# A two-layer diffusion backbone on one core: a gated tile's low part cut and moved, half of the last head's transposed blocks in other buffers, a gate tile loaded later

## The chip, the cores and the metric

The kernel runs on one core of one Trainium2 chip. The metric is the device time of one execution in microseconds (us). TensorE (PE in the profile) multiplies matrices, VectorE (DVE), ScalarE (ACT) and GpSimd (POOL) work element by element, SyncE (SP) issues the transfers between the chip's main memory and the on-chip memory (SBUF). Matmul results stand in PSUM, which is cut into banks of 512 fp32 columns on 128 partitions. Each engine runs its own instructions in their order, and semaphores order the engines among each other.

## The reference

Each of two layers modulates and normalizes the input, projects it once to all queries, keys, values and gates, runs two attentions side by side, and merges them:

```python
def _merge(a_att, b_att, a_z, b_z, g_a, g_b, w_o_a, w_o_b, w_out):
    o_a = (a_att * jax.nn.silu(a_z)) @ w_o_a
    o_b = (b_att * jax.nn.silu(b_z)) @ w_o_b
    merged = jax.nn.sigmoid(g_a) * o_a + jax.nn.sigmoid(g_b) * o_b
    return merged @ w_out
...
    a_att = _na_latent(qa, ka, va, cka, cva, rpb, rows)
...
    b_att = _gqa_latent(qb, k_all, v_all)
    out_x = _merge(a_att, b_att, a_z, b_z, g_a, g_b, w_o_a, w_o_b, w_out)
    x_new = x + gate_x * out_x
```

`_na_latent` is a neighbourhood attention with 8 heads, `_gqa_latent` a full attention with 8 query heads on 2 key/value heads. There are 512 latent tokens and 256 context tokens of width 1024, heads of 64. Layer 0 also updates the context (768 tokens in all); layer 1 does not, and gives the 512 latent tokens out. All is fp32.

## The kernel before

**Numbers in two parts.** Every fp32 operand of a large product is split into a high part (cast to a TensorE format, on ACT) and a low part (the difference, on DVE or POOL). One product is three matmuls: high by high (L352), high by low and low by high (L353, L354 in either role). `mm3` issues them. A slab of weights is loaded into a staging buffer `raw` (three of them), cast into `whi` on ACT and subtracted into `wlo` on DVE or POOL in turn; `load_w2` (L327 to L341) does that for 256 columns, two rows of 128 at once. `whi` and `wlo` are rings of eight buffers each, handed out in program order and shared by all weights.

**The second attention.** `pipeline` runs eight heads. For head h it makes the scores (L719, L720, banks `pss`: a ring of two of 1024 columns), the softmax (exponent L958 on ACT, the division L657 on DVE or L659 and L660 on POOL), and then the values of head h-1 (`gq_values`). The values of a head need the softmax result transposed: in six blocks of 128 keys, `transpose_split` sets four transposes (L670) into one bank of a ring of two (`pst`, kind "t"), casts the block's high part into `pth` on ACT (L673) and subtracts its low part into `ptl` on DVE (L674); two buffers of each. Two matmuls per block (L973, L974) add up in the one bank `psv`. `head_out` then copies half of it to a single buffer `ho` on ACT (L682), adds the other half on DVE (L683), and multiplies the result into the gate tile `zb` on POOL (L684), which makes it the second gated tile. In layer 0 the 256 context queries go through the same path (L747, L748).

**What fills the gaps.** Between heads the pipeline issues pieces of other work from a list: gate projections and the first branch's output projection with `w_o_a` (psf matmuls with `gah` and `gal`, evacuated at L593).

**The end of a layer's attention.** When the eight heads' scores are issued, `early()` (L985) loads two gate tiles, `tg[1]` and `tg[3]`, takes two large buffers for the second gated tile's parts (`gbh`, `gbl`; from `big`, a ring of nine buffers of 128x3072), and splits three quarters of it by `hilo` (L555: cast L558 on ACT, subtraction L559 on POOL). Then come the last head's values. Then the merge takes the PSUM banks anew (five of a kind "x" beside "f"), loads the output gate, splits the last quarter, and runs over four chunks of `w_o_b`: `chunks[i][0]()` loads two slabs of weights, `chunks[i][1]` holds the matmuls (psf and psx with `gbh`, `gbl`) and `evac_b` (L1006), which joins both branches in the gate tiles and splits the result into `mh` and `ml`. After it, `w_out` multiplies that (loaded by `load_w`, L317 to L326).

**What sets the order.** The program gives the instructions in the order above; a scheduler then sets each engine's order by its own planned times, and buffers of a ring are handed out in program order, each when the reader of what stood in it before is done. So the changed kernel's order on each engine isn't read from the code, but from the built program.

Of the kernel before, what the change touches and what calls it, by code (L numbers as in the profile page):

```python
# [9 lines left out]
F32R = mybir.dt.float32r  # L10
BF16 = mybir.dt.bfloat16
AF = mybir.ActivationFunctionType
ALU = mybir.AluOpType
# [46 lines left out]
def R(ap):  # L60
    return ap.bitcast(F32R)
# [7 lines left out]
def hybrid_kernel(es: ExitStack, tc, x, ctx, cvec, w_ada, w_ada0, small, gvec, w_in, w_o_a, w_o_b, w_out,  # L69
                  bias_int, bias_edge, rope, ident_d, out):  # L70
    nc = tc.nc
    V, S, G, T = nc.vector, nc.scalar, nc.gpsimd, nc.tensor
# [3 lines left out]
    wp = es.enter_context(tc.tile_pool(name="wp", bufs=8))  # L76
# [6 lines left out]
    def nm(s):  # L83
        uid[0] += 1
        return f"{s}_{uid[0]}"

    def big(name):
        return bigp.tile([128, 3072], F32, tag="big", name=nm(name))
# [23 lines left out]
    def psw(n=512, kind="w"):  # L112
        if kind == "w":
            kind = "f" if pm["i"] % pm["n"] == 0 else "x"
            pm["i"] += 1
        pool, cols = pm[kind]
        return pool.tile([128, cols], F32, tag=kind, name=nm("ps" + kind))[:, :n]
# [290 lines left out]
    def run(fill, n):  # L408
        for _ in range(min(n, len(fill))):
            fill.pop(0)()  # L410
# [80 lines left out]
    def layer(l, hx, nxt, mid):  # L491
# [60 lines left out]
        def hilo_tiles(name):  # L552
            return [big(name + part).rearrange("p (f n) -> p f n", f=4) for part in "hl"]

        def hilo(src, dst, fs):  # L555
            sv = src.rearrange("p (f n) -> p f n", f=4)
            for f in fs:
                S.copy(R(dst[0][:, f, :ntok]), sv[:, f, :ntok])  # L558
                G.tensor_tensor(R(dst[1][:, f, :ntok]), sv[:, f, :ntok], dst[0][:, f, :ntok], ALU.subtract)  # L559

        def load_tg(c):
            nc.sync.dma_start(tg[c].rearrange("p (f n) -> p f n", f=4)[:, :, :ntok], gs[c][:, :, :ntok])
# [88 lines left out]
        if True:  # L651
# [10 lines left out]

            def transpose_split(blocks, n0=0, n1=512):

                pt = psw(512, "t")
                for src, c0 in blocks:
                    if c0 is None:
                        T.transpose(pt.rearrange("p (s n) -> p s n", n=64)[:, 0:8:7, :], src, ident)
                    else:
                        T.transpose(pt[:, c0:c0 + 128], src, ident)  # L670
                hi = att["p"].tile([128, 512], F32R, tag="pth", name=nm("pth"), bufs=att["nt"])
                lo = att["p"].tile([128, 512], F32R, tag="ptl", name=nm("ptl"), bufs=att["nt"])
                S.copy(hi[:, n0:n1], pt[:, n0:n1])  # L673
                V.tensor_tensor(lo[:, n0:n1], pt[:, n0:n1], F(hi[:, n0:n1]), ALU.subtract)  # L674
                return hi, lo

            def head_out(po, e, dst):

                n = dst.shape[-1]
                m, o = 64 * e, 64 * (1 - e)  # L680
                t1 = att["p"].tile([128, 512], F32, tag="ho", name=nm("ho"), bufs=1)
                S.copy(t1[m:m + 64, :n], po[o:o + 64, :n])  # L682
                V.tensor_tensor(t1[m:m + 64, :n], po[m:m + 64, :n], t1[m:m + 64, :n], ALU.add)  # L683
                G.tensor_tensor(dst, dst, t1[m:m + 64, :n], ALU.mult)  # L684

            def rows(a, half):
                return a[64 * half:64 * half + 64]
# [150 lines left out]
            def pipeline(fill, spread, scores_of, values_of, last=None, bg=[]):  # L838

                n = len(fill)  # L840
                prev = None
                for h in range(8):
                    att["bg"] = bg if h > 3 or pm["n"] == 1 else []
                    st = scores_of(h)
                    if prev is not None:
                        values_of(h - 1, prev)
                    run(fill, len(fill) - (n - n * min(h + 1, spread) // spread))
                    prev = st
                if last is not None:
                    run(fill, len(fill))  # L850
                    last()
                run(bg, len(bg))
                values_of(7, prev)
                run(fill, len(fill))

            akt = [k_tile(e, True) for e in range(2)]

            def na_first(h):
                j, e = h // 2, h % 2
# [6 lines left out]
            def values_of(dst, f):  # L866
                def g(h, st):
                    vsl = f(h, st[0])
                    if first:
                        e = h % 2  # L870
                        zv = dst.rearrange("p (f n) -> p f n", f=4)
                        ctx_values(st[1], vsl, zv[64 * e:64 * e + 64, h // 2, 512:768], e)
                return g
# [110 lines left out]

            def early():  # L985

                for c in (1, 3):
                    tg[c] = big("tg")
                    load_tg(c)
                gated["b"] = hilo_tiles("gb")  # L990
                hilo(zb, gated["b"], range(3))
            bg = gate_steps((1,), att["p"]) if first else []
# [3 lines left out]
        with tc.tile_pool(name=f"mrg{l}", bufs=1, reuse_waits="tile") as mp:  # L996
# [3 lines left out]
            for v in range(nv):  # L1000
                src = gd[l][8 * v:8 * v + 8].rearrange("k p -> (k p)").unsqueeze(0)
                nc.sync.dma_start(gv[:, v, :], src.to_broadcast([128, DM]))
            hilo(zb, gated["b"], [3])
            mg = []

            def evac_b(f, n0, n1, ps):  # L1006
# [8 lines left out]
            for i in range(4):  # L1015
                if i < 3:
                    chunks[i + 1][0]()
                if i % 2 == 0:
                    mg.append(hilo_tiles("m"))
                for piece in chunks[i][1]:  # L1020
                    piece()
# [225 lines left out]
```

## Time and profile before

| | us |
|---|---|
| three runs of before | 1146.18, 1144.71, 1144.48 (median 1144.71) |
| the profiled execution | 1144.91 |
| its span in the profile | 1143.1 |
| idle time of DVE before `ptl` L674, all 176 of the kernel | 43.4 |
| idle time of ACT before `pth` L673, all 176 | 93.2 |

The span is what the profile records from the first instruction to the last; 1.8 us of the profiled execution lie around it. A row of the timeline has the start, the duration, the engine, the line, the operation, what is written and from what, the shape and the count, and in brackets the idle time ahead of it with the engine and the tile that ended it. A matmul's recorded duration overlaps the next one's, so two starts tell more than a duration. The kernel has 6128 matmuls and transposes, and the context part of layer 1 is left out by the reference itself.

### The profile page before, as it was taken

How to read it: one execution, taken by the hardware profiler on the slowest of the kernel's cores; microseconds unless marked ns; L12 is line 12 of the kernel's file. 1: busy time of each engine (PE TensorE's matmuls, PEld its weight loads, DVE VectorE, ACT ScalarE, POOL GpSimd, SP SyncE). 2: the span in 40 equal slices, each digit the busy share in tenths (PEclk: the TensorE clock that was granted, in tenths of full speed). 3: DMA queues.
4: the chain of work that ended last, by engine and by line, in shares of the span. 5: the costliest groups of instructions: out<-in, count | busy, mean ns of one | idle time of the engine just before them, and what ended most of it. 6: DMA issues, size and time to landing. Idle time of an engine off the chain costs nothing.

```text
span 1143.1 us, 17425 instructions
## 1 busy us (share of the span) xinstructions
PE 1120.7 (98%) x6128; PEld 947.6 (83%) x6128; DVE 816.3 (71%) x1535; ACT 581.4 (51%) x1185; POOL 480.6 (42%) x449
## 2 busy tenths in 40 slices
PE   7999999999999999999999999999999999999998
PEld 5788888888988888888788787888887888887787
DVE  6777688887554786697588655469777665898573
ACT  6553366665443565666330355337666355766521
POOL 1073354553364333453511226345453664465311
PEclk9999999999999999999999999999999999999999
DMA  9645212333323232451434424633332333152133
GB/s 368 241 123 157 85 56 70 99 116 97 118 94 97 96 101 86 98 217 38 152 124 134 148 69 122 186 103 116 99 114 65 111 103 102 65 175 92 64 126 97
DMA packets 91886, 135.08 MB, mean 118 GB/s; under 512 B 10804, under 2 KB 55064, under 8 KB 91160
## 3 DMA queue, kind: packets, MB, share of 16 engines
q1 hardware_dynamic: 91520, 133.87, 36.9%
q8 instruction: 48, 0.79, 0.3%
q14 instruction: 38, 0.31, 0.1%
q10 hardware_dynamic: 280, 0.12, 0.0%
HBM read 116.63 MB, written 17.32 MB: 117 GB/s over the span
## 4 chain that ended last, share of the span: by engine, by line
PE 87%; DVE 5%; DMA 2%; ACT 2%; issue 2%; POOL 1%; SPq 0%; ACTq 0%; POOLq 0%; DVEq 0%
PE psx L352 12%; PE psx L354 12%; PE psx L353 12%; PE psf L352 10%; PE psf L353 10%; PE psf L354 10%; PE pst L670 5%; PE pss L792 3%; PE pss L719 2%; PE pss L720 2%; PE psv L974 2%; PE psv L973 1%; PE pst L432 1%; DVE ptl L674 1%; DMA rawb<-in_w_ada_dram 1%
## 5 line engine op out<-in xcount | busy, mean ns | idle before, releaser
L674 DVE TENSOR_TENSOR ptl<-pst,pth 128x512 fp32r<-128x512 f32 (+1 forms) x176 | 115.9, 671 | 43.4 <-ACT pth L673 42.4
L673 ACT CAST pth<-pst 128x512 fp32r<-128x512 f32 (+1 forms) x176 | 99.2, 577 | 93.2 <-PE pst L670 53.1
L352 PE MATMUL psf<-hx,whi 128*128 128x512 f32 (+1 forms) x368 | 140.1, 381 | 0.1
L339 POOL TENSOR_TENSOR wlo<-raw,whi 128x512 fp32r<-128x512 f32 x68 | 95.9, 1414 | 103.5 <-ACT whi L337 86.2
L353 PE MATMUL psf<-hx,whi 128*128 128x512 f32 (+1 forms) x368 | 138.0, 375 | 0.0
L354 PE MATMUL psf<-hx,wlo 128*128 128x512 f32 (+1 forms) x368 | 137.6, 374 | 0.0
L352 PE MATMUL psx<-whi,hx 128*128 128x512 f32 (+1 forms) x368 | 137.6, 375 | 0.0
L354 PE MATMUL psx<-whi,hx 128*128 128x512 f32 (+1 forms) x368 | 135.8, 369 | 0.0
L353 PE MATMUL psx<-wlo,hx 128*128 128x512 f32 (+1 forms) x368 | 135.7, 369 | 0.0
L337 ACT CAST whi<-raw 128x512 fp32r<-128x512 f32 x136 | 82.8, 620 | 51.3 <-DMA raw<-in_w_in_dram 32.5
L322 ACT CAST whi<-raw 128x512 fp32r<-128x512 f32 x88 | 53.9, 622 | 100.5 <-PE psx L354 38.3
L670 PE MATMUL pst<-ident,p 128*128 128x128 f32 x640 | 99.5, 272 | 1.4 <-DVE ptl L674 0.9
L325 POOL TENSOR_TENSOR wlo<-raw,whi 128x512 fp32r<-128x512 f32 x36 | 49.5, 1378 | 119.6 <-ACT whi L322 106.2
L339 DVE TENSOR_TENSOR wlo<-raw,whi 128x512 fp32r<-128x512 f32 x68 | 68.0, 1001 | 32.1 <-ACT whi L337 31.6
L670 PEld LDWEIGHTS pst<-ident,p 128*128 128x128 f32 x640 | 77.8, 141 | 13.4 <-DVE ptl L674 1.3
L660 POOL TENSOR_TENSOR p<-p,r 128x512 f32<-128x512 f32 (+1 forms) x64 | 83.5, 1305 | 4.9
L659 POOL TENSOR_SCALAR r<-r 128x1 f32<-128x1 f32 x64 | 22.2, 347 | 150.4 <-DVE r L654 126.9
L352 PEld LDWEIGHTS psx<-whi,hx 128*128 128x128 f32 x368 | 69.5, 189 | 12.3 <-issue 0.8
L354 PEld LDWEIGHTS psx<-whi,hx 128*128 128x128 f32 x368 | 69.4, 189 | 11.9
L354 PEld LDWEIGHTS psf<-hx,wlo 128*128 128x128 f32 x368 | 69.3, 188 | 11.7
L353 PEld LDWEIGHTS psx<-wlo,hx 128*128 128x128 f32 x368 | 69.5, 189 | 10.7
L352 PEld LDWEIGHTS psf<-hx,whi 128*128 128x128 f32 x368 | 69.4, 189 | 10.5 <-ACT zt L517 0.3
(253 smaller groups left out, 3049.7 us busy)
## 6 DMA issues: line engine op xcount, KB each, us to landing
raw<-in_w_in_dram SPq DMA_DIRECT2D x168, 256.0 KB, 2.9
rawb<-in_w_ada_dram SPq DMA_DIRECT2D x64, 256.0 KB, 2.8
gs<-zt SPq DMA_DIRECT2D x32, 256.0 KB, 2.0
raw<-in_w_out_dram SPq DMA_DIRECT2D x32, 256.0 KB, 2.9
tg<-gs SPq DMA_DIRECT2D x4, 1536.0 KB, 6.8
rawx<-in_w_ada_dram SPq DMA_DIRECT2D x8, 512.0 KB, 7.7
raw<-in_w_o_a_dram SPq DMA_DIRECT2D x16, 256.0 KB, 2.7
raw<-in_w_o_b_dram SPq DMA_DIRECT2D x16, 256.0 KB, 3.3
```

The source lines that it names most:

```text
L322: S.copy(hi[:, :n], raw[:, :n])
L325: e.tensor_tensor(lo[:, :n], raw[:, :n], F(hi[:, :n]), ALU.subtract)
L337: S.copy(hi, raw)
L339: lo_eng(i).tensor_tensor(lo, raw, F(hi), ALU.subtract)
L352: T.matmul(ps, lhs[0], rhs[0], start=first, stop=False)
L353: T.matmul(ps, lhs[0], rhs[1], start=False, stop=False)
L354: T.matmul(ps, lhs[1], rhs[0], start=False, stop=last)
L660: G.tensor_tensor(p[:, c0:c1], p[:, c0:c1], r[:, i:i + 1].to_broadcast([128, c1 - c0]), ALU.mult)
L670: T.transpose(pt[:, c0:c0 + 128], src, ident)
L673: S.copy(hi[:, n0:n1], pt[:, n0:n1])
L674: V.tensor_tensor(lo[:, n0:n1], pt[:, n0:n1], F(hi[:, n0:n1]), ALU.subtract)
L792: T.matmul(pss.rearrange("p (a b n) -> p a b n", a=2, b=2), qi, blocks_of(k, *at), start=b, stop=not b)
```

## The change

Four edits. (1) `hilo` may cut a quarter into stretches of columns and put the low part on another engine; the last quarter of the second gated tile is cut into 0 to 512 and 512 to 768 in layer 0 (one stretch in layer 1), low part on DVE. (2) For the last head of layer 1, every second transposed block goes into a score bank, and its two parts into the weights' ring `whi`, `wlo`. (3) The last head's product into `zb` runs on DVE, in both layers and for the context rows too. (4) `tg[3]` is taken from the large ring and loaded after the first two chunks of `w_o_b` are, so `gbh` and `gbl` take the buffers one place earlier in that ring.

```diff
--- before.py
+++ after.py
@@ -552,11 +552,12 @@
         def hilo_tiles(name):
             return [big(name + part).rearrange("p (f n) -> p f n", f=4) for part in "hl"]
 
-        def hilo(src, dst, fs):
+        def hilo(src, dst, fs, parts=None, lo=G):
             sv = src.rearrange("p (f n) -> p f n", f=4)
             for f in fs:
-                S.copy(R(dst[0][:, f, :ntok]), sv[:, f, :ntok])
-                G.tensor_tensor(R(dst[1][:, f, :ntok]), sv[:, f, :ntok], dst[0][:, f, :ntok], ALU.subtract)
+                for a, b in parts or [(0, ntok)]:
+                    S.copy(R(dst[0][:, f, a:b]), sv[:, f, a:b])
+                    lo.tensor_tensor(R(dst[1][:, f, a:b]), sv[:, f, a:b], dst[0][:, f, a:b], ALU.subtract)
 
         def load_tg(c):
             nc.sync.dma_start(tg[c].rearrange("p (f n) -> p f n", f=4)[:, :, :ntok], gs[c][:, :, :ntok])
@@ -662,14 +663,17 @@
 
             def transpose_split(blocks, n0=0, n1=512):
 
-                pt = psw(512, "t")
+                spare = att["end"] and not first and att["turn"] % 2 == 1
+                att["turn"] += 1
+                pt = psw(512, "s" if spare else "t")
                 for src, c0 in blocks:
                     if c0 is None:
                         T.transpose(pt.rearrange("p (s n) -> p s n", n=64)[:, 0:8:7, :], src, ident)
                     else:
                         T.transpose(pt[:, c0:c0 + 128], src, ident)
-                hi = att["p"].tile([128, 512], F32R, tag="pth", name=nm("pth"), bufs=att["nt"])
-                lo = att["p"].tile([128, 512], F32R, tag="ptl", name=nm("ptl"), bufs=att["nt"])
+                pool, th, tl, n = (wp, "whi", "wlo", 8) if spare else (att["p"], "pth", "ptl", att["nt"])
+                hi = pool.tile([128, 512], F32R, tag=th, name=nm(th), bufs=n)
+                lo = pool.tile([128, 512], F32R, tag=tl, name=nm(tl), bufs=n)
                 S.copy(hi[:, n0:n1], pt[:, n0:n1])
                 V.tensor_tensor(lo[:, n0:n1], pt[:, n0:n1], F(hi[:, n0:n1]), ALU.subtract)
                 return hi, lo
@@ -681,7 +685,7 @@
                 t1 = att["p"].tile([128, 512], F32, tag="ho", name=nm("ho"), bufs=1)
                 S.copy(t1[m:m + 64, :n], po[o:o + 64, :n])
                 V.tensor_tensor(t1[m:m + 64, :n], po[m:m + 64, :n], t1[m:m + 64, :n], ALU.add)
-                G.tensor_tensor(dst, dst, t1[m:m + 64, :n], ALU.mult)
+                (V if att["end"] else G).tensor_tensor(dst, dst, t1[m:m + 64, :n], ALU.mult)
 
             def rows(a, half):
                 return a[64 * half:64 * half + 64]
@@ -850,10 +854,12 @@
                     run(fill, len(fill))
                     last()
                 run(bg, len(bg))
+                att["end"] = last is not None
                 values_of(7, prev)
                 run(fill, len(fill))
 
             akt = [k_tile(e, True) for e in range(2)]
+            att["end"], att["turn"] = False, 0
 
             def na_first(h):
                 j, e = h // 2, h % 2
@@ -984,9 +990,8 @@
 
             def early():
 
-                for c in (1, 3):
-                    tg[c] = big("tg")
-                    load_tg(c)
+                tg[1] = big("tg")
+                load_tg(1)
                 gated["b"] = hilo_tiles("gb")
                 hilo(zb, gated["b"], range(3))
             bg = gate_steps((1,), att["p"]) if first else []
@@ -1000,7 +1005,7 @@
             for v in range(nv):
                 src = gd[l][8 * v:8 * v + 8].rearrange("k p -> (k p)").unsqueeze(0)
                 nc.sync.dma_start(gv[:, v, :], src.to_broadcast([128, DM]))
-            hilo(zb, gated["b"], [3])
+            hilo(zb, gated["b"], [3], spans, V)
             mg = []
 
             def evac_b(f, n0, n1, ps):
@@ -1015,6 +1020,9 @@
             for i in range(4):
                 if i < 3:
                     chunks[i + 1][0]()
+                if i == 0:
+                    tg[3] = big("tg")
+                    load_tg(3)
                 if i % 2 == 0:
                     mg.append(hilo_tiles("m"))
                 for piece in chunks[i][1]:
```

In the rows below a line number of the changed kernel is 4 to 8 higher than that of the same line before (L559 for L558, L677 for L673, L339 is the same), and the numbers of tiles shift by a few.

ScalarE at the end of layer 1's heads, before the change. `pth` is the high part of a transposed block (pth_11664 to 11697: the seventh head, 11767 to 11822: the last), `gbh` the gated tile's third quarter, `ho` the copy of a finished head.

```order
L558 CAST gbh_11753<-zb_10277 128x512
L673 CAST pth_11675<-pst_11670 128x512
L673 CAST pth_11686<-pst_11681 128x512
L673 CAST pth_11697<-pst_11692 128x512
L673 CAST pth_11767<-pst_11762 128x512
L682 COPY ho_11703<-psv_11636 64x512
L673 CAST pth_11778<-pst_11773 128x512
L673 CAST pth_11789<-pst_11784 128x512
L673 CAST pth_11800<-pst_11795 128x512
L673 CAST pth_11811<-pst_11806 128x512
L673 CAST pth_11822<-pst_11817 128x512
```

The same place after the change; `whi` from `pss` is a transposed block in the weights' ring, `whi` from `raw` a slab of `w_o_b`.

```order
L559 CAST gbh_11753<-zb_10279 128x512
L677 CAST pth_11677<-pst_11672 128x512
L677 CAST whi_11822<-pss_11817 128x512
L337 CAST whi_11847<-raw_11845 128x512
L337 CAST whi_11853<-raw_11851 128x512
L337 CAST whi_11859<-raw_11857 128x512
L677 CAST pth_11688<-pst_11683 128x512
L677 CAST pth_11699<-pst_11694 128x512
L337 CAST whi_11865<-raw_11863 128x512
L337 CAST whi_11909<-raw_11907 128x512
L677 CAST pth_11767<-pst_11762 128x512
L686 COPY ho_11705<-psv_11638 64x512
```

The last head's second, fourth and sixth block moved ahead of the seventh head's last two blocks, and the casts of the first five slabs of `w_o_b`, before spread through the heads, now stand between them and the last head's first block.

VectorE at the same place before the change: the low parts `ptl`, the heads' additions `ho`, and then the first low part of `w_out`.

```order
L674 TENSOR_TENSOR ptl_11768<-pst_11762,pth_11767 128x512
L683 TENSOR_TENSOR ho_11703<-psv_11636,ho_11703 64x512
L674 TENSOR_TENSOR ptl_11779<-pst_11773,pth_11778 128x512
L674 TENSOR_TENSOR ptl_11790<-pst_11784,pth_11789 128x512
L674 TENSOR_TENSOR ptl_11801<-pst_11795,pth_11800 128x512
L674 TENSOR_TENSOR ptl_11812<-pst_11806,pth_11811 128x512
L674 TENSOR_TENSOR ptl_11823<-pst_11817,pth_11822 128x512
L683 TENSOR_TENSOR ho_11828<-psv_11761,ho_11828 64x512
L325 TENSOR_TENSOR wlo_12049<-raw_12045,whi_12047 128x512
```

And after it, with `wlo` from `raw` the low part of a `w_o_b` slab:

```order
L339 TENSOR_TENSOR wlo_11867<-raw_11863,whi_11865 128x512
L678 TENSOR_TENSOR ptl_11768<-pst_11762,pth_11767 128x512
L687 TENSOR_TENSOR ho_11705<-psv_11638,ho_11705 64x512
L678 TENSOR_TENSOR ptl_11790<-pst_11784,pth_11789 128x512
L678 TENSOR_TENSOR ptl_11812<-pst_11806,pth_11811 128x512
L339 TENSOR_TENSOR wlo_11917<-raw_11913,whi_11915 128x512
L339 TENSOR_TENSOR wlo_11963<-raw_11959,whi_11961 128x512
L687 TENSOR_TENSOR ho_11828<-psv_11761,ho_11828 64x512
L688 TENSOR_TENSOR zb_10279<-zb_10279,ho_11828 64x512
L560 TENSOR_TENSOR gbl_11754<-zb_10279,gbh_11753 128x512
```

Three low parts of blocks went away from here (they stand earlier), three of slabs came in, and behind the last addition stand the product into `zb` and the low part of the gated tile's last quarter, which were on GpSimd.

TensorE at the end of layer 0's heads, before the change: psf are the merge's matmuls with the gated tile, psv the last head's values, pst a transposed block of the context, psv_6413 the context's values.

```order
L352 MATMUL psf_6462<-gbh_6325,whi_6438 128x512
L973 MATMUL psv_6333<-pth_6383,vb_3516 128x512
L353 MATMUL psf_6462<-gbl_6326,whi_6438 128x512
L354 MATMUL psf_6462<-gbh_6325,wlo_6440 128x512
L352 MATMUL psf_6462<-gbh_6325,whi_6438 128x512
L974 MATMUL psv_6333<-ptl_6384,vb_3516 128x512
L973 MATMUL psv_6333<-pth_6394,vb_3516 128x512
L670 MATMUL pst_6404<-ident,p_6155 128x128 x4
L974 MATMUL psv_6333<-ptl_6395,vb_3516 128x512
L353 MATMUL psf_6462<-gbl_6326,whi_6438 128x512
L354 MATMUL psf_6462<-gbh_6325,wlo_6440 128x512
L352 MATMUL psf_6462<-gbh_6325,whi_6444 128x512
```

After the change:

```order
L352 MATMUL psf_6464<-gbh_6323,whi_6444 128x512
L353 MATMUL psf_6464<-gbl_6324,whi_6444 128x512
L354 MATMUL psf_6464<-gbh_6323,wlo_6446 128x512
L979 MATMUL psv_6331<-pth_6381,vb_3516 128x512
L980 MATMUL psv_6331<-ptl_6382,vb_3516 128x512
L979 MATMUL psv_6331<-pth_6392,vb_3516 128x512
L673 MATMUL pst_6402<-ident,p_6155 128x128 x4
L980 MATMUL psv_6331<-ptl_6393,vb_3516 128x512
L751 MATMUL psv_6411<-pth_6407,vb_3516 128x256
L752 MATMUL psv_6411<-ptl_6408,vb_3516 128x256
L751 MATMUL psv_6411<-pth_6407,vb_3516 128x256
L752 MATMUL psv_6411<-ptl_6408,vb_3516 128x256
```

Nine matmuls of psf (the last three of them are the first rows here) stand ahead of the last three value matmuls and of the transposes; before, they stood between and behind them.

## The prediction

> **What bounds the kernel now.** I read the page's totals and its chain of waits first, then the busy time of each engine by stretches, then the rows of the two places that the change touches.
>
> ```profile
> span 1143.1 us, 17425 instructions
> PE 1120.7 (98%) x6128; PEld 947.6 (83%) x6128; DVE 816.3 (71%) x1535; ACT 581.4 (51%) x1185; POOL 480.6 (42%) x449
> PE 87%; DVE 5%; DMA 2%; ACT 2%; issue 2%; POOL 1%; SPq 0%; ACTq 0%; POOLq 0%; DVEq 0%
> ...
> core 0: us, PE busy (x) PEld busy (x) DVE busy (x) ACT busy (x) POOL busy (x), PEclk, DMA share, GB/s
> 540.00:567.00 27.00, 25.01 (x151) 21.22 (x150) 12.88 (x21) 9.81 (x17) 14.29 (x10) 1.00 0.36 119
> 1000.00:1053.00 53.00, 52.73 (x282) 43.85 (x281) 48.46 (x73) 34.98 (x69) 29.61 (x28) 1.00 0.39 134
> 1053.00:1075.00 22.00, 19.21 (x102) 13.72 (x101) 14.28 (x21) 11.80 (x22) 9.89 (x8) 1.00 0.18 54
> ```
>
> TensorE sets the time: 98% busy, 87% of the chain, at a granted clock of 1.00 in these stretches. The change removes none of its instructions, so all that can be gained is its idle time. That is small nearly everywhere (0.27 us in the 53 us before 1053), and 2.79 us by the records in the stretch from 1053 to 1075, the last heads of layer 1. Records of matmuls overlap, so I measure by starts instead. These rows give the pitch:
>
> ```profile
> 1075.04 0.40 PE L352 MATMUL psx<-gbh,whi 128*128 128x512 f32 x1
> ...
> 1080.52 0.39 PE L352 MATMUL psf<-gbh,whi 128*128 128x512 f32 x1
> ```
>
> Between these two starts lie 24 matmuls of 512 columns: 5.48/24 = 0.228 us each. A group of four transposes holds TensorE 0.35 us (554.43 to 554.78 below), a 256-column matmul 0.12 (558.62 to 558.74 below). From 1053.3 to 1075.04 TensorE issues 41 such matmuls and 14 groups: 41 x 0.228 + 14 x 0.355 = 14.3 us of work in 21.7. **Some 7.4 us are lost there**, and no other place that the change touches is as large.
>
> **Layer 0: the second gated tile's new buffer.** The old rows:
>
> ```profile
> 552.43 0.48 PE L352 MATMUL psf<-gbh,whi 128*128 128x512 f32 x1
> ...
> 554.43 0.60 PE L670 MATMUL pst<-ident,p 128*128 128x128 f32 x4
> 554.78 0.48 PE L974 MATMUL psv<-ptl,vb 128*128 128x512 f32 x1
> ...
> 556.75 0.50 PE L353 MATMUL psf<-gbl,whi 128*128 128x512 f32 x1 [0.79 <-POOL gbl L559]
> ...
> 558.62 0.28 PE L353 MATMUL psx<-gbl,whi 128*128 128x256 f32 x1
> 558.74 0.28 PE L354 MATMUL psx<-gbh,wlo 128*128 128x256 f32 x1
> 560.22 0.50 PE L352 MATMUL psx<-gbh,whi 128*128 128x512 f32 x1 [1.21 <-DVE ho L683]
> ...
> 555.07 0.59 ACT L673 CAST pth<-pst 128x512 fp32r<-128x512 f32 x1 [1.76 <-PE pst L670]
> 555.68 0.58 ACT L682 COPY ho<-psv 64x512 f32<-64x512 f32 x1
> ...
> 555.69 0.69 DVE L674 TENSOR_TENSOR ptl<-pst,pth 128x512 fp32r<-128x512 f32 x1 [1.28 <-ACT pth L673]
> 556.41 0.69 DVE L683 TENSOR_TENSOR ho<-psv,ho 64x512 f32<-64x512 f32 x1
> ...
> 529.10 1.31 POOL L684 TENSOR_TENSOR zb<-zb,ho 64x512 f32<-64x512 f32 x1 [4.12 <-DVE ho L683]
> ...
> 550.82 5.87 POOL L559 TENSOR_TENSOR gbl<-zb,gbh 128x768 fp32r<-128x768 f32 x3 [3.60 <-PE psf L353]
> 558.03 1.28 POOL L684 TENSOR_TENSOR zb<-zb,ho 64x512 f32<-64x512 f32 x1
> ```
>
> From 552.43 to 560.22 TensorE has 13 matmuls of 512 columns (2.96), one group of transposes (0.36), and 13 matmuls of 256 (1.55): 4.87 us of work in 7.79, so 2.9 lost. The three low parts of the gated tile start only at 550.82, because their buffers came free there; under the change they stand right behind the product at 529.10, and the wait of 0.79 on them goes. What is late next? In the changed order nine of the merge's matmuls stand in front of the last transposes, so these start at 552.43 + 12 x 0.228 = 555.2, later than before. From the rows: transposes to cast 0.64, cast to the next ACT instruction 0.61, ACT's copy to DVE's add 0.73, and an add to the matmul that waits for its bank 0.74 (the 1054.88 row to the 1055.62 row below). The one output bank is free at 555.2 + 0.64 + 0.61 + 0.73 + 0.74 = 557.9. TensorE has nothing from 555.8: a wait of 2.1. Eight 256-column matmuls later (558.9) stands the first one that needs the tile's last quarter. Its chain: add until 557.85, product now on VectorE (priced by the add of the same 64x512 shape, 0.69; on GpSimd it took 1.28), to 558.6, the cast behind the context copy, ready at about 559.6: a wait of 0.7. So 2.1 + 0.7 = 2.8 lost against 2.9: **nothing gained**. Bounds: a gain of 2.9 if both waits had other cover; against it
>
> ```profile
> 530.41 0.60 DVE L657 TENSOR_SCALAR p<-p,r 128x768 f32<-128x768 f32 x1
> ```
>
> two low parts (5.87/3 = 1.96 each) would now run beside this step of the softmax: up to 0.5 lost, as none of it has a cover of 1 us; I take -0.2.
>
> **Layer 1, up to 1053: o_b's weights leave the heads.** The spare blocks take three slots of the weights' ring of eight, in program order ahead of o_b's eight slabs, which therefore go behind them: eight casts on ACT (0.63 each by the 1050.86 row below), four subtractions on DVE and four on GpSimd leave the heads.
>
> ```profile
> 1018.08 1.77 DVE L339 TENSOR_TENSOR wlo<-raw,whi 128x512 fp32r<-128x512 f32 x1
> ...
> 1025.16 0.50 PE L352 MATMUL psf<-gah,whi 128*128 128x512 f32 x1 [0.23 <-DVE tg L593]
> ...
> 1050.86 0.63 ACT L337 CAST whi<-raw 128x512 fp32r<-128x512 f32 x1
> ```
>
> DVE is 91% busy there (48.46 of 53), and TensorE's waits on it are few (the 0.23 here and a like one). Bounds 0 and 1.0; I take 0.6, most of those waits.
>
> **Layer 1, 1053 to 1075.**
>
> ```profile
> 1053.21 1.75 DVE L339 TENSOR_TENSOR wlo<-raw,whi 128x512 fp32r<-128x512 f32 x1
> 1054.88 1.27 DVE L674 TENSOR_TENSOR ptl<-pst,pth 128x512 fp32r<-128x512 f32 x2
> 1075.90 0.69 DVE L683 TENSOR_TENSOR ho<-psv,ho 64x512 f32<-64x512 f32 x1 [1.26 <-ACT ho L682]
> 1081.15 0.69 DVE L325 TENSOR_TENSOR wlo<-raw,whi 128x512 fp32r<-128x512 f32 x1 [4.55 <-ACT whi L322]
> ...
> 1055.62 0.50 PE L974 MATMUL psv<-ptl,vb 128*128 128x512 f32 x1 [1.54 <-DVE ptl L674]
> ...
> 1052.95 1.46 POOL L660 TENSOR_TENSOR p<-p,r 128x768 f32<-128x768 f32 x1
> ...
> 1063.77 1.28 POOL L559 TENSOR_TENSOR gbl<-zb,gbh 128x512 fp32r<-128x512 f32 x1 [0.73 <-ACT gbh L558]
> ...
> 1078.00 0.62 ACT L558 CAST gbh<-zb 128x512 fp32r<-128x512 f32 x1 [2.13 <-POOL zb L684]
> ...
> raw<-in_w_o_b_dram SPq DMA_DIRECT2D x8, 256.0 KB, 3.7
> ...
> DMA to landing us min/median/max: 2.5/2.6/4.9
> ```
>
> First, the slab's subtraction of 1.75 in front of the transposed blocks moves away, and TensorE's wait of 1.54 with it. Second, three of the last head's six blocks no longer queue for two banks: a block through a bank takes 0.64 + 0.62 + 0.74 plus its transposes, 2.35 us, so two banks pass one each 1.2 us, while TensorE's work on it is 0.81 (0.355 + 2 x 0.228). In the replay with these four latencies the waits on banks, 7.4 - 1.54 = 5.9 before, come to 3.3: 2.6 less. Third, what comes back: the slabs' work now stands among the last heads. On ACT the casts of the fourth and fifth slab stand ahead of the last head's first cast. Their staging buffer (one of three) comes free only when GpSimd has subtracted an earlier slab. I replayed the new order with these durations: the gated tile's third low part (1063.77) comes 1.5 earlier, as TensorE's wait of 1.54 is gone, and ends near 1063.6; the slab's subtraction behind it takes 1.3, to 1064.9. The load then lands 2.6 later (the median of staging loads in 1040 to 1100), so ACT, and behind it TensorE, stands still for 2.25. Before that, the merge's first matmuls wait 0.8 for the first slab's low part, which stands behind the gated tile's third on GpSimd. So -1.54 - 2.6 + 0.8 + 2.25 = **-1.1 us**: the start at 1075.04 comes at 1073.9. Fourth, behind it ACT has three more casts and DVE two more subtractions (0.69 each) ahead of the last head's add, which frees a bank that the merge's next matmuls want: 0.55 lost (between 0.4 and 1.4, the latter where both subtractions take like 1.75). The last quarter of the gated tile is cast at 1078.00 and first read at 1080.52 now; with the product and low part on VectorE (0.69 and 0.69 for 1.29 and 1.29) it is no later, and hides under the 24 matmuls. From there on TensorE's work is dense and the same. SyncE: the load of the other gate tile is queued between the third and fourth slab, and its buffer is free long before; it costs the fourth slab's landing nothing that I can see, at most one issue of a third of a microsecond.
>
> The 1.75 row ran beside a GpSimd instruction on SBUF (1052.95), the 0.69 of the same shape (1081.15) beside none. [...]
>
> **Sum.** Layer 0 -0.2, heads +0.6, last heads +1.1, bank -0.55: a gain of 0.95, say 1.0 us. Against the profiled execution, 1144.91 (span 1143.1 and 1.8 around it), 1143.9; the median of the runs, 1144.71, lies 0.2 lower, so **1143.7**.
>
> **Rivals.**
> Faster than a measurement can tell apart from none (0.2%, 2.3 us): the fourth and fifth slab land in time, as when GpSimd subtracts the earlier one sooner; then 2.25 us of the wait is not paid and the gain is 3.2, 1141.5. Likewise if layer 0's wait of 2.1 is covered. For it: it takes only one slab moved by two instructions; against: the order on ACT is fixed. Chance 0.27.
> Slower than before: the round trip of a staging buffer (subtraction, issue, landing) takes longer than 2.6, as the eight o_b loads of before did (median 3.7, longest in the window 4.9). Two such trips stand in line ahead of the last head, so each microsecond more counts twice: nothing is left of the gain from 3.1 us (0.95/2 more), it is 2.3 us slower than before from 4.2, and at 4.9 the time is 1148.4. For it: 3.7 would already give +1.25 (1146.0). Against: that median was taken while much else was loaded (134 GB/s), and these loads find 54. Chance 0.15.
> The change does in sum nothing: the two subtractions ahead of the last head's add take 1.75 each instead of 0.69, the bank's wait is 1.4 instead of 0.55, and 0.1 is left: 1144.6. Chance 0.13.
> My forecast, gain 0 to 2: 0.45.
>
> **How the numbers follow.** The likeliest is 1143.7. The range reaches to the faster rival with a little beyond, 1140.8 (3.9 gained), and in the slower one to a landing of 4.0, 1146.6. Faster by over 0.2%: the first rival 0.27; slower by over 0.2%: the landings beyond 4.2 and mishaps of that size, 0.11; within: 0.62.
>
> **What would show it.** In the changed profile: no 1.5 us wait of TensorE on DVE near 1053 and the start of the merge matmuls that stood at 1075.04 about 1.5 earlier (0.6 + 1.1 - 0.2); ACT's wait on a staging load of o_b with TensorE idle about 2 us beside it, some 5 us earlier than that; in layer 0 low parts at 530 instead of 550 and a wait on DVE of about 2 near 556 in place of the two of before. I am wrong in the layer 0 step if that wait is missing, in the slab step if ACT's casts find their loads landed, and in the heads' step if the last heads begin no sooner.

## The result, and the profile after

| | median, us | lowest to highest | runs |
|---|---|---|---|
| before | 1144.96 | 1144.48 to 1146.18 | 4 |
| changed | 1153.39 | 1152.14 to 1154.24 | 4 |

The ratio is 1.0069 (95% interval 1.0057 to 1.0082): 8.4 us slower by the medians, where 1.0 us less had been forecast. The stated range ended at 1146.6.

The page of the changed kernel:

```profile
span 1152.4 us, 17421 instructions
PE 1123.8 (98%) x6128; PEld 952.2 (83%) x6128; DVE 825.2 (72%) x1541; ACT 582.4 (51%) x1186; POOL 473.7 (41%) x444
PEclk9999999999999999999999999999999999998899
PE 89%; DVE 4%; DMA 4%; ACT 2%; issue 1%; POOL 1%; SPq 0%; ACTq 0%; POOLq 0%
```

The span grew by 9.3 us. The row of the clock, all nines before, has two eights, and DMA's share of the chain doubled. To find the place, take the start of the n-th matmul, counted from 0, in both traces (both have 6128, and nearly everywhere in the same order); the last column is changed minus before:

| n-th matmul | before, us | changed, us | difference |
|---|---|---|---|
| 3000 | 518.52 | 518.48 | -0.04 |
| 3100 (last heads, layer 0) | 534.78 | 535.78 | +1.00 |
| 3300 (merge, layer 0) | 570.22 | 571.41 | +1.19 |
| 5550 (heads, layer 1) | 1019.27 | 1020.07 | +0.80 |
| 5720 | 1052.05 | 1051.90 | -0.15 |
| 5800 | 1069.04 | 1072.96 | +3.92 |
| 5900 (merge, layer 1) | 1092.08 | 1101.33 | +9.25 |
| 6127 | 1138.53 | 1147.79 | +9.26 |

So 1.0 us goes in layer 0's last heads, 0.95 comes in layer 1's heads, and then 4.1 and 5.3 go in two steps. The stretches around these two steps, with the busy time of each engine and the granted clock:

```profile
core 0: us, PE busy (x) PEld busy (x) DVE busy (x) ACT busy (x) POOL busy (x), PEclk, DMA share, GB/s
1049.60:1056.60 7.00, 4.17 (x24) 3.27 (x22) 6.39 (x6) 2.34 (x6) 5.39 (x5) 1.00 0.45 150
1056.70:1063.40 6.70, 5.84 (x23) 4.99 (x23) 2.95 (x6) 2.37 (x5) 1.68 (x2) 0.50 0.00 0
1063.50:1077.10 13.60, 10.05 (x58) 7.63 (x57) 8.42 (x12) 8.27 (x17) 5.60 (x5) 1.00 0.19 60
1077.20:1083.90 6.70, 5.63 (x16) 4.58 (x17) 3.34 (x5) 3.29 (x6) 3.21 (x3) 0.50 0.37 108
```

Each step is a stretch in which TensorE stands idle, followed by one in which it is busy at half the clock. The first one, by the timelines of TensorE, VectorE and GpSimd:

```profile
1053.30 0.47 PE L979 MATMUL psv<-pth,vb 128*128 128x512 f32 x1
1057.56 0.79 PE L980 MATMUL psv<-ptl,vb 128*128 128x512 f32 x1 [3.79 <-DVE ptl L678]
...
1051.00 4.45 DVE L658 TENSOR_SCALAR p<-p,r 128x768 f32<-128x768 f32 x1
1056.83 0.68 DVE L678 TENSOR_TENSOR ptl<-pst,pth 128x512 fp32r<-128x512 f32 x1
...
1050.90 0.21 POOL L660 TENSOR_SCALAR r<-r 128x1 f32<-128x1 f32 x1
1051.07 2.53 POOL L560 TENSOR_TENSOR gbl<-zb,gbh 128x512 fp32r<-128x512 f32 x2
1053.57 1.46 POOL L661 TENSOR_TENSOR p<-p,r 128x768 f32<-128x768 f32 x1
```

VectorE's division of one block of the softmax (L658) took 4.45 us. Meanwhile GpSimd ran the gated tile's first two low parts and its own division without a pause, to 1055.03; VectorE's division ended at 1055.45. The same place in the kernel before:

```profile
1051.21 0.62 DVE L657 TENSOR_SCALAR p<-p,r 128x768 f32<-128x768 f32 x1
...
1051.06 0.20 POOL L659 TENSOR_SCALAR r<-r 128x1 f32<-128x1 f32 x1
1051.56 1.42 POOL L339 TENSOR_TENSOR wlo<-raw,whi 128x512 fp32r<-128x512 f32 x1 [0.30 <-PE pst L670]
1052.95 1.46 POOL L660 TENSOR_TENSOR p<-p,r 128x768 f32<-128x768 f32 x1
1054.38 2.95 POOL L559 TENSOR_TENSOR gbl<-zb,gbh 128x512 fp32r<-128x512 f32 x2
```

There GpSimd paused for 0.30 us behind its scaling (L659), VectorE's division took 0.62, and the two low parts came behind GpSimd's division. In the changed kernel they moved ahead of it, without that pause, because their buffers came free earlier (the later tile alone, below, moves them too).

The second step, by the timelines of TensorE and ScalarE, and what the staging buffer's transfers took between 1060 and 1084:

```profile
1073.63 0.60 PE L673 MATMUL pst<-ident,p 128*128 128x128 f32 x4
1078.27 1.12 PE L673 MATMUL pst<-ident,p 128*128 128x128 f32 x4 [4.04 <-DVE ptl L678]
1081.74 0.63 PE L979 MATMUL psv<-whi,vb 128*128 128x512 f32 x1
1082.17 0.63 PE L980 MATMUL psv<-wlo,vb 128*128 128x512 f32 x1
...
1075.75 1.25 ACT L337 CAST whi<-raw 128x512 fp32r<-128x512 f32 x2 [4.63 <-DMA raw<-in_w_o_b_dram]
1076.91 0.58 ACT L677 CAST pth<-pst 128x512 fp32r<-128x512 f32 x1
...
DMA to landing us min/median/max: 2.6/4.7/4.8
```

ScalarE's casts of the fourth and fifth slab stand ahead of the last head's first cast and wait 4.63 us for their load, which took 4.7. TensorE stands idle 4.04 and then has a pitch of 0.43 us (1081.74 to 1082.17), not 0.23.

Layer 0, by TensorE, VectorE and GpSimd:

```profile
559.00 0.39 PE L751 MATMUL psv<-pth,vb 128*128 128x256 f32 x1 [1.90 <-DVE ho L687]
560.83 0.50 PE L352 MATMUL psf<-gbh,whi 128*128 128x512 f32 x1 [0.63 <-ACT gbh L559]
...
532.34 2.33 DVE L658 TENSOR_SCALAR p<-p,r 128x256 f32<-128x256 f32 x2
...
530.43 4.09 POOL L560 TENSOR_TENSOR gbl<-zb,gbh 128x768 fp32r<-128x768 f32 x2
```

Here too low parts on GpSimd stand beside VectorE's divisions. Two of 128x256 took 2.33, in place of 0.61 before:

```profile
534.05 0.61 DVE L657 TENSOR_SCALAR p<-p,r 128x256 f32<-128x256 f32 x2
```

### The profile page after: what moved, and what is told of

Its sections match the earlier page's. It is cut to its first block, busy times and chain, and to the rows that moved or that the text cites. A ratio compares the mean times of both kernels' runs of the same rounds, so it can differ in the third digit from the quotient of the medians.

```text
span 1152.4 us, 17421 instructions
## 1 busy us (share of the span) xinstructions
PE 1123.8 (98%) x6128; PEld 952.2 (83%) x6128; DVE 825.2 (72%) x1541; ACT 582.4 (51%) x1186; POOL 473.7 (41%) x444
## 4 chain that ended last, share of the span: by engine, by line
PE 89%; DVE 4%; DMA 4%; ACT 2%; issue 1%; POOL 1%; SPq 0%; ACTq 0%; POOLq 0%
PE psx L352 12%; PE psx L353 12%; PE psx L354 12%; PE psf L352 10%; PE psf L353 10%; PE psf L354 10%; PE pst L673 5%; PE pss L796 2%; PE pss L723 2%; PE pss L724 2%; PE psv L980 2%; PE psv L979 2%; PE pst L432 1%; DMA gs<-zt 1%; DMA rawb<-in_w_ada_dram 1%
## 5 line engine op out<-in xcount | busy, mean ns | idle before, releaser
L677 ACT CAST pth<-pst 128x512 fp32r<-128x512 f32 (+1 forms) x173 | 97.3, 577 | 101.5 <-PE pst L673 61.4
L339 POOL TENSOR_TENSOR wlo<-raw,whi 128x512 fp32r<-128x512 f32 x68 | 95.5, 1408 | 106.0 <-ACT whi L337 85.6
L673 PE MATMUL pst<-ident,p 128*128 128x128 f32 x628 | 99.5, 276 | 4.6 <-DVE ptl L678 4.0
L339 DVE TENSOR_TENSOR wlo<-raw,whi 128x512 fp32r<-128x512 f32 x68 | 68.2, 1004 | 39.2 <-ACT whi L337 37.5
L673 PEld LDWEIGHTS pst<-ident,p 128*128 128x128 f32 x628 | 77.7, 143 | 16.5 <-DVE ptl L678 4.3
```

The source lines that it names most:

```text
L339: lo_eng(i).tensor_tensor(lo, raw, F(hi), ALU.subtract)
```

## The experiments

The theory after this reading: the loss is two idle stretches with separate causes (GpSimd's run in VectorE's way, from the later tile; the slab's load, from the spare blocks in the weights' ring), and each costs about as much again in clock. Times are medians, each against the kernel before on the same chip.

| run | this, us | before, us | ratio (95%) |
|---|---|---|---|
| later tile alone | 1151.54 | 1145.34 | 1.0054 (1.0039 to 1.0069) |
| spare blocks alone | 1147.17 | 1145.34 | 1.0016 (1.0006 to 1.0026) |
| last head on VectorE alone | 1145.85 | 1145.34 | 1.0001 (0.9992 to 1.0011) |
| changed, no spare blocks | 1154.07 | 1145.34 | 1.0074 (1.0059 to 1.0089) |
| changed, low parts on VectorE | 1150.99 | 1145.03 | 1.0044 (1.0030 to 1.0058) |
| changed, own buffers | 1150.42 | 1145.24 | 1.0046 (1.0028 to 1.0064) |
| changed, both mended | 1148.02 | 1145.03 | 1.0022 (1.0013 to 1.0031) |
| spare blocks, wait filled | 1145.81 | 1145.03 | 1.0006 (0.9997 to 1.0014) |
| later tile, layer 0 alone | 1147.10 | 1144.73 | 1.0014 (1.0005 to 1.0023) |
| both mended, layer 0 filled | 1147.86 | 1144.73 | 1.0025 (1.0015 to 1.0035) |
| spare blocks, own buffers | 1143.00 | 1145.03 | 0.9980 (0.9971 to 0.9990) |
| the same, last slab on GpSimd | 1142.19 | 1144.73 | 0.9974 (0.9965 to 0.9983) |

**The later tile alone** has edit 4 only:

```diff
-                for c in (1, 3):
-                    tg[c] = big("tg")
-                    load_tg(c)
+                tg[1] = big("tg")
+                load_tg(1)
...
+                if i == 0:
+                    tg[3] = big("tg")
+                    load_tg(3)
```

> Before, with only the later load of the second gate tile (edit 4). Theory: in layer 1 the gated tile's first two low parts now stand on GpSimd right behind the scaling that is released by the same reciprocals as VectorE's division of 128x768, with a weight slab and a division behind them, so VectorE's division waits for a run of GpSimd instructions: 4 to 6 us instead of 0.6, TensorE idle 4 us or more near 1053, then a granted clock of 0.5 for 6.8 us; in layer 0 about 1 us of the same. Time 1149 to 1153. Rival (the long division comes from the transfers of the spare blocks' slabs): the division stays at 0.6, time within 1 us of before, about 1145.

It lost 6.2 us. VectorE and GpSimd near 1054:

```profile
1053.70 5.68 DVE L657 TENSOR_SCALAR p<-p,r 128x768 f32<-128x768 f32 x1
...
1053.81 2.52 POOL L559 TENSOR_TENSOR gbl<-zb,gbh 128x512 fp32r<-128x512 f32 x2
1056.29 1.25 POOL L339 TENSOR_TENSOR wlo<-raw,whi 128x512 fp32r<-128x512 f32 x1
1057.51 1.46 POOL L660 TENSOR_TENSOR p<-p,r 128x768 f32<-128x768 f32 x1
```

One instruction more in GpSimd's run (a slab's low part, 1.25) makes the division longer by 1.23. The theory holds but for the clock's part: half clock came for 3.4 us in layer 1, not 6.8, and for 3.4 us in layer 0. The rival that the spare blocks' transfers are to blame falls.

**The spare blocks alone** have edit 2 only (the spare branch of `transpose_split` in the change's diff, and the flag that turns it on).

> Before, with only the spare blocks in score banks and the weights' ring (edit 2). Theory: ScalarE's casts of the fourth and fifth slab wait over 4 us for their load ahead of the last head, TensorE is idle 4 us and then runs 6.8 us at a clock of 0.5, +5.3 us; if a low part of the gated tile comes behind the scaling on GpSimd here too, the long division comes on top. Time 1149 to 1154. Rival (the trip is only long because the last heads began late, after the other stall): ScalarE waits about 2 us, no half clock there, time 1144 to 1146.

It lost 1.8 us, less than expected, because the spare blocks gained first: TensorE was 2.7 us ahead of before at the 5750th matmul and 2.8 behind at the 5900th. In between ScalarE waited 4.91 for a slab's load and TensorE 4.33, and half clock followed for 6.8 us. The wait does not need the other loss. The division was not held, though low parts stand near it, and the rows show why:

```profile
1050.53 0.62 DVE L657 TENSOR_SCALAR p<-p,r 128x768 f32<-128x768 f32 x1
...
1050.91 1.39 POOL L559 TENSOR_TENSOR gbl<-zb,gbh 128x512 fp32r<-128x512 f32 x1 [0.33 <-PE pst L672]
1052.26 1.46 POOL L660 TENSOR_TENSOR p<-p,r 128x768 f32<-128x768 f32 x1
```

GpSimd's low part waited 0.33 for TensorE here, as the slab's low part did before (0.30), and the division got through in 0.62.

**The last head on VectorE alone** has edits 1 and 3.

> Before, with only the last head's product and the last quarter's low part on VectorE, cut in layer 0 (edits 1 and 3). Theory: off the critical path in layer 1, under 1 us gained in layer 0: 1144 to 1145. Rival (work moved to VectorE is a part of the loss): 1146 or more.

No difference by the ratio (1.0001; the medians lie 0.5 apart, with the ranges overlapping). The product and the low part on VectorE neither cost nor bring anything; the small gain expected in layer 0 did not come.

**The changed kernel without the spare blocks** (edits 1, 3 and 4):

> The changed kernel without the spare blocks (edits 1, 3 and 4). Theory: as with the later tile alone, the long division, idle TensorE and 6.8 us of half clock near 1053, no wait for a slab's load later: 1148 to 1153. Rival (both losses need the spare blocks): 1144 to 1146.

It lost 8.7 us, a little more than was expected: the division took 5.71, and in the profiled execution 6.8 us of half clock came in layer 0 as well, and 3.4 in layer 1.

**The low parts of layer 1 on VectorE**, in the changed kernel:

```diff
-                hilo(zb, gated["b"], range(3))
+                hilo(zb, gated["b"], range(3), None, G if first else V)
```

> The changed kernel with the gated tile's first three low parts of layer 1 on VectorE instead of GpSimd. Theory (a run of GpSimd instructions keeps VectorE's division out): the division near 1051 takes 0.6 to 1.5 us instead of 4.45, no wait of TensorE above 2 us and no half clock near 1053, about 4 us less than the changed kernel; the wait for a slab's load with its half clock stays: 1148 to 1150. Rival (the division is long for another reason, such as the tile's load that runs then): it stays over 4 us, 1153.

It is 2.4 us below the changed kernel, though 4 were expected. VectorE and GpSimd near 1054:

```profile
1054.61 1.82 DVE L658 TENSOR_SCALAR p<-p,r 128x768 f32<-128x768 f32 x1
...
1054.24 1.78 POOL L661 TENSOR_TENSOR p<-p,r 128x768 f32<-128x768 f32 x1
```

The division is held by one instruction only, and there is no half clock near 1053. From the 5720th matmul to the 5800th it lost 0.5 us on before, the changed kernel 4.1. Of these 3.6 us, 1.6 were given back in layer 0, where the profiled execution of this kernel has 3.4 us of half clock and that of the changed kernel none.

**The changed kernel with buffers of their own for the spare blocks**, so that the slabs keep their places:

```diff
-                pool, th, tl, n = (wp, "whi", "wlo", 8) if spare else (att["p"], "pth", "ptl", att["nt"])
+                th, tl, n = ("sph", "spl", 2) if spare else ("pth", "ptl", att["nt"])
+                pool = att["p"]
```

> The changed kernel with the spare blocks' parts in two buffers of their own, and the low parts left on GpSimd. Theory: no wait for a slab's load, but the division waits again, and for one instruction more (a slab's low part stands in GpSimd's run here): 5.7 us, ending 0.4 us behind the run's end; half clock in layer 1 once, not twice; 1148 to 1151. Rival (the long division needs the spare blocks' slabs, the loss is one cause): division under 2 us, 1144 to 1146.

No wait for a load, and the division at 5.68 (1053.42 to 1059.10, GpSimd's run ending at 1058.68); one half clock in layer 1, of 3.4 us, and one of the same length in layer 0. It is 3.0 us below the changed kernel. So with either cause mended alone a loss of 5 to 6 us stays.

**Both mended**: own buffers, and the first three low parts on VectorE in both layers.

> All four edits, with the spare blocks' parts in two buffers of their own and the gated tile's first three low parts on VectorE in both layers. Theory: both causes are gone, layer 0's later wait of 1.9 us stays and may cost a half clock of 3.4 us there; 1142 to 1146, at least 7 us below the changed kernel. Rival (the low parts on VectorE delay its own work by as much): 1149 or more.

The loss fell from 8.4 us to 3.0, but was not gone; 7 us less had been expected, it is 5.4. What is left lies in layer 0 (1.6 in the profiled execution, with 3.4 us of half clock) and in the last heads of layer 1 (1.6 from the 5720th matmul to the 5740th), where the rows show that the first cause is moved and not gone:

```profile
1053.45 3.97 DVE L560 TENSOR_TENSOR gbl<-zb,gbh 128x512 fp32r<-128x512 f32 x2
1057.35 0.61 DVE L658 TENSOR_SCALAR p<-p,r 128x768 f32<-128x768 f32 x1
...
1054.16 1.29 POOL L339 TENSOR_TENSOR wlo<-raw,whi 128x512 fp32r<-128x512 f32 x1
1055.41 1.46 POOL L661 TENSOR_TENSOR p<-p,r 128x768 f32<-128x768 f32 x1
```

The two low parts, now on VectorE and in front of its division, took 3.97 beside GpSimd's run (1.27 in the kernel with layer 1's low parts on VectorE), and the division behind them took 0.61.

**The later tile in layer 0 alone:**

> Before, with the later load of the second gate tile in layer 0 alone (edit 4 for one layer). Theory: in layer 0 VectorE's divisions near 532 wait for GpSimd's run (about 1 us lost), and TensorE's wait of 1.9 us near 557 stays and brings 3.4 us of half clock in many executions: 1.5 to 2.5 us slower than before, mean clock 0.997 to 0.999; layer 1 as before. Rival (layer 0 is even, as the prediction had it): within 0.7 us of before.

It lost 2.4 us by the medians, 1.6 by the ratio, with layer 1 as before. The rival (layer 0 even) falls. Its eleven executions go from 1145.21 us, at a mean clock of 1.000, to 1147.78, at 0.998; the wait of 1.90 for the output bank is in the profiled one, and behind it the stretch from 561.07 to 564.48 has half the clock.

**The spare blocks with the wait filled**: 16 matmuls more in the second half of a score bank that nobody reads, where TensorE waits. The lines that issue them:

```diff
+                    if not first and h == 7 and k == 5:
+                        for _ in range(16):
+                            T.matmul(att["full"][:, 512:1024], vsl(0), att["late"], start=True, stop=True)
```

> The spare-block kernel (edit 2 alone) with 16 matmuls more, about 3.7 us, whose result is not read, placed where TensorE waits for the slab's load. Theory (half of the loss there is the clock, which falls because TensorE stood idle): the wait is as long, but the clock stays 1.0 behind it, and the time is 2.5 to 3 us below the spare-block kernel: 1144 to 1145. Rival (the matmuls behind the wait are slow for another reason, or the extra matmuls only add): 1147 or more.

TensorE, in the place of the wait, and the pitch behind it:

```profile
1066.68 3.92 PE L985 MATMUL pss<-ptl,vb 128*128 128x512 f32 x16
1070.43 0.60 PE L675 MATMUL pst<-ident,p 128*128 128x128 f32 x4
...
1072.26 0.39 PE L986 MATMUL psv<-whi,vb 128*128 128x512 f32 x1
1072.49 0.40 PE L987 MATMUL psv<-wlo,vb 128*128 128x512 f32 x1
```

The same matmuls now have a pitch of 0.23, and the clock is 0.999 or 1.000 in all eleven executions; it was 0.997 or 0.998 in all ten of the spare blocks alone. More work, and 1.4 us less by the medians; against each one's own kernel before it is 1.0 (0.8 lost for 1.8), since the two were timed on different chips, and the intervals of the two ratios overlap. In the profiled executions the loss on before from the 5750th matmul to the last is 2.7 us instead of 5.5 (the 16 not counted), of which some 0.8 is a shorter wait: ScalarE waited 3.68 for the slab's load here and 4.91 there, and the transposes on both sides of the wait start 4.10 us apart instead of 4.93. So the clock's share is about 2.0 us by this working, and less by the medians; 2.5 to 3 had been expected. That the half clock comes from the idle time is shown, its size is not.

**Both mended, layer 0 filled** with nine such matmuls in the wait of 1.9 us:

> The mended kernel with all four edits, and nine matmuls more (2.1 us) whose result is not read, where TensorE waits 1.9 us for the output bank at the end of layer 0's heads. Theory (that wait costs the clock in part of the executions): clock 0.999 or 1.0 in all of them, the time 1 to 1.5 us below the mended kernel, 1146.3 to 1147.2, and a smaller spread. Rival (the spread comes from elsewhere): 1148 or more, clock still down to 0.996.

A miss. Layer 0 kept its clock in the profiled execution, but 3.4 us of half clock came in layer 1 (1058.8 to 1062.2), and the median is the same as without (1147.86, 1148.02). Layer 1 has a wait of 2.2 us in both kernels (2.20 here, 2.21 in the one without the filling), and only here did half clock follow it; the last section shows why. Filling one of several waits does not settle the time.

**The spare blocks with own buffers** on the kernel before, without the other edits:

> Before, with the spare blocks in score banks but their two parts in two buffers of their own, so that the slabs of w_o_b keep their places in the weights' ring. Theory: no wait of ScalarE on a slab's load, no half clock, and the spare blocks' own gain stays, 1.5 to 2.7 us: 1142.5 to 1144. Rival (the gain that the spare-block kernel showed ahead of its wait came from the slabs that had left the heads, not from the banks): within 0.7 of before, 1144.5 to 1146.

2.0 us faster. At the 5700th matmul it is 0.06 ahead of before, at the 5900th 2.56: the spare blocks bring 2.5 us where nothing pushes the slabs.

**The same with the last slab on GpSimd** in layer 1:

```diff
-                    st["w"] = load_w2(src, 256 * i, 4, mix_lo)
+                    st["w"] = load_w2(src, 256 * i, 4, pool_lo if br == "b" and i == 3 and not first else mix_lo)
```

> Before, with the spare blocks' parts in two buffers of their own, and the last slab of w_o_b in layer 1 subtracted on GpSimd instead of VectorE. Theory (that slab's 1.75 us on VectorE is TensorE's wait of 1.54 near 1055): 1.0 to 1.5 us below the own-buffer kernel, 1141.3 to 1142.2. Rival (GpSimd then is late with the next division or low part): as the own-buffer kernel, 1143, or slower.

2.5 us faster than before, and the fastest kernel of the study. The stretch of the last heads, which had 19.21 us of TensorE busy before:

```profile
1053.00:1075.00 22.00, 20.75 (x116) 16.12 (x115) 13.01 (x21) 12.01 (x23) 11.89 (x10) 1.00 0.21 73
```

From the 5720th matmul to the 5750th it gains 1.4 on before, the kernel with own buffers 0.45: 1.0 for that slab at its place. Between the medians it is 0.8, and 0.5 against each one's own kernel before.

## Why the prediction was wrong

**Right in mechanism, and near in size.** The slabs that leave layer 1's heads: 0.6 forecast, 0.95 measured. The spare blocks' gain and the slab's wait of 1.54 on VectorE: 2.6 and 1.54, 4.1 together, forecast; 3.1 measured from the 5700th matmul to the 5900th where both causes of loss are absent (the last kernel): 2.5 with the blocks alone, and 0.5 to 1.0 by the slab. Layer 0's new waits: 2.1 and 0.7 forecast, 1.90 and 0.63 measured. The last head's product and low part on VectorE: nothing, as forecast.

**The step that failed first** is the layer 1 sum, "-1.54 - 2.6 + 0.8 + 2.25 = -1.1": it has no term for the first two low parts, which moved there as they did in layer 0. The prediction looked at such neighbours in layer 0 only ("up to 0.5 lost"; it took -0.2), where the last heads lost 1.0, and layer 0 as a whole 1.2. In layer 1 GpSimd's run, which these two low parts lengthened, held VectorE's division for 4.45 us, and TensorE 3.79: where the prediction had 1.1 gained, the last heads lost 4.1 up to the 5800th matmul, before the slab's wait came. The kernels with the later tile alone and with own buffers show it without the other cause, and the one with layer 1's low parts on VectorE shows it gone but for 0.5. The prediction had a row of the same kind at hand (a slab's subtraction of 1.75 beside GpSimd, 0.69 alone), but weighed it for the two subtractions ahead of the last head's add only.

**A term that was mis-sized**: TensorE's wait on the slab's load, 2.25 forecast and 4.04 measured, because the load took 4.7 and not 2.6. Three loads of slabs go out there within 1.2 us (1071.05 to 1072.21) and took 4.67 to 4.84, and the next one, issued at 1077.12, took 2.61; the 2.6 was the median of all staging loads from 1040 to 1100 in the trace before. That it is their number that makes them slow was not tested. The second rival had named a landing of up to 4.9 as the less likely case; it let each microsecond count twice, and here 2.1 us more of landing made 1.8 more of waiting.

**A term that was left out**: the clock. The prediction priced each wait at its own length. In the changed kernel's profiled execution two stretches of 6.8 us ran at 0.50, in which TensorE had work from 1057.56 to 1063.49 and from 1078.27 to 1083.97; half of these 5.9 and 5.7 us, 5.8 us in all, is more than half of the 9.3. This is an estimate: for the spare blocks alone the same working gives 2.4, and filling the wait gave back 2.0 at most. The half-clock stretches in which TensorE had work are 3.4 or 6.8 us long in these traces, and in layer 0 one followed a wait of 1.90 us (the later tile in layer 0 alone). By the limit that the traces show (last section), the waits that were forecast, 2.1 and 2.25 us, could have brought half clock too.

The bank's wait of 0.55 that was forecast behind the three late casts did not come: the merge's first matmul starts 9.12 us later than before (1084.16 against 1075.04), and the 5900th 9.25, so 0.13 was lost between them.

Still open: the exact share of the clock in the medians, since only the profiled executions show which stretches ran at half clock; why the three loads took 4.7; and what would remain of the later tile if GpSimd were given a pause ahead of the low parts, which was not tried.

## What to carry over

When a buffer comes free earlier, look at who starts earlier for it and on which engine it then runs beside whom: here a gain of buffers moved two GpSimd instructions into the pause of 0.30 us in which VectorE's division had slipped through. Where TensorE is 98% busy, a wait of some 4 us is not priced at its own length: here it cost some 2 to 3 us more in clock, by estimate. Borrowing slots of a ring moves its regular users behind the borrower, with their loads: two small buffers of its own turned the same idea from 1.8 us lost into 2.0 gained.

## What the hardware showed that was not expected

VectorE's division of 128x768 (a tensor by a scalar of each partition) ended 0.41 to 0.42 us behind the end of GpSimd's unbroken run in five kernels, whatever the length of the run: 1055.45 after 1055.03 (changed), 1059.38 after 1058.97 (later tile alone), 1059.10 after 1058.68 (own buffers), 1060.53 after 1060.11 (no spare blocks), 1056.43 after 1056.02 (low parts on VectorE). In these five it did not end before GpSimd's run did, over up to four instructions that GpSimd began after it (later tile alone: two low parts, a slab's and the division, 1053.81 to 1058.97). With a pause of 0.30 us (before) and 0.33 us (spare blocks alone) behind GpSimd's scaling it took 0.62. What keeps it waiting inside the run was not shown.

The granted clock changed on a grid in these traces, and whether half clock followed a wait went with how much of it lay within one step. In each of the fourteen traces any two changes of the granted clock lie a whole number of steps of 3.413 us apart; in the changed kernel's they stand at 1056.67, 1063.49, 1077.15, 1083.97 and 1152.24, which are 2, 4, 2 and 20 steps. Cut each trace into these steps, from 15 us on, and add up TensorE's idle time in each by its records:

| step | steps | TensorE idle in it, us |
|---|---|---|
| at full clock, the next one too | 4582 | 0 to 1.72 |
| at full clock, the next one at half | 26 | 1.90 to 3.41 |
| at half clock, the next one at half | 4 | 0.60 to 2.01 |
| at half clock, the next one at full | 14 | 0 to 0.37 |

So the limit lies between 1.72 and 1.90 us idle in one step in these traces, and a half clock lasted until a step with at most 0.37 us idle. By this the same wait cost the clock in one execution and not in another. The 1.90 us of layer 0 lay within one step in the later tile in layer 0 alone (557.66 to 561.07), and half clock followed; in the changed kernel the grid cut them at 558.32, the two steps had 1.22 and 1.31 us idle in all, and none followed. In the same way the 2.2 us of layer 1 lay within one step with layer 0 filled (2.20) and were cut in both mended (1.19 and 1.21).
